# New places for background steps and a new order of attention's blocks in a two-network kernel

## The chip, the cores and the metric

The kernel runs on one core of one Trainium2 chip. The metric is device time in microseconds (us) of one execution, and the median of several executions is quoted. The trace was taken in one further execution, whose own time stands beside its span.

The engines are named as in the profile: PE (TensorE: matmuls and transposes), DVE (VectorE), ACT (ScalarE), POOL (GpSimd) and SP (SyncE, which issues most DMAs).

## What is computed

Two small networks run one after the other on 512 tokens of width 1024, all in float32. The first has a pooling mixer, a feed-forward layer, attention over a window of 128 tokens with shared keys and values, and a second feed-forward layer. The second network (an S5 mixer, an MLP, a state-space mixer, an MLP, a final norm) takes its output. Cut to what matters here:

```python
def conv_glu_ffn(h, w_in, conv_w, conv_b, w_out):          # twice: layer 0 and layer 1
    u = h @ w_in                                           # 1024 -> 2 x 2816
    u = sum(conv_w[k] * up[:, k:k + S] for k in range(3)) + conv_b
    gate, val = jnp.split(u, 2, axis=-1)
    return (gelu(gate) * val) @ w_out                      # 2816 -> 1024

def swa_sink_attention(q, kk, vv, sinks):                  # between the two
    s = einsum('bnqhgd,bnkhd->bnhgqk', q, kk)              # 4 token blocks x 4 groups of 4 heads
    p = exp(where(valid, s, -1e30) - m)
    return einsum('bnhgqk,bnkhd->bnqhgd', p, vv) / denom

# and for the second network, ahead of its time:
mod = silu(c) @ ada_w[0] + ada_b[0]                        # 1024 x 6144, one row
tables = f(s5_lambda, s5_log_dt, s5_b, s5_c, s5_d)         # the S5 mixer's tables, per group of states
```

## The kernel before

**Matmuls.** Each float32 product is made as three matmuls: activations and weights are split into a high and a low part (`hi`, `lo`; `wh`, `wl`). Weights come by DMA in chunks of 4 x 128 rows by 256 columns into `ws` (three buffers), ACT copies `wh` (L205) and DVE makes `wl` (L206), four buffers each. The matmuls are L220 to L222. PSUM tiles `mm` have four buffers.

**Feed-forward layer** (`ffn_layer`, L960). The 22 column tiles of the hidden width go in three phases, tiles 0 to 7, 8 to 15 and 16 to 21. In a phase each block of two tiles runs 96 matmuls of 512 columns for gate and value (tiles `h`), and then `glu`: DVE scales the four PSUM tiles (`u`, L969), ACT and DVE do the convolution (L974 to L976), ACT the gelu, DVE the product (L983) and the low part `lo` (L321). Tiles 0 and 1 are done ahead of the body. After the first and the second phase a down-projection (`project`) adds the phase's share of the output in four pairs of column tiles, and `evac` is called eight times. The third phase's down-projection is the layer's tail; it is done in two token halves of 256 columns, between which the next layer's norm is interleaved.

**Background.** `bg[0](n)` takes n steps of each generator that is registered (class `Background`). In layer 0 that is `s5_tables` (lines L560 to L793): it has 14 steps of small work, then, for each of 8 group blocks, two steps of phasors (L681 to L683) and five of matrices (L725 to L764), with a store (L780 to L793: ACT copies, PE transposes and matmuls `pb`, DMAs on ACT's queue) for each half of a group block. In layer 1 there are two generators, `ada_units` (two loads of 256 KB on POOL's queue, L495, and two DVE multiplies, L500, a step) and `s5_toeplitz`, short. What is left behind the body is drained at once: `end_tables` in layer 0, `work.drain()` in layer 1.

Steps are called at the body's start (2), after each block (`rate`: 5 in layer 0, 4 in layer 1) and after each evacuation of a down-projection (1).

**Attention** (`attention_layer`, `body_`). Sixteen blocks (g, n), g a group of four heads and n a block of 128 tokens. A block has `scores` (PE L1195 into the one buffer `sc`; DVE mask add L1198, maximum L1203, small ones L1204 and L1205; ACT exponentials L1207; DVE sum and reciprocal L1209 and L1210; POOL normalisation L1211), `turn` two blocks later (PE transposes L1219, copies to `pT`) and `values` three blocks later (PE L1237; `oh` and `ol`). `order` lists them: all groups with token blocks 0 and 1, then all with 2 and 3. Between the blocks `filler` takes steps of other PE work, as many as ATT_F says for that block: 12 steps of the query projections of groups 1 to 3 (`q_proj`, each a chunk of 12 matmuls of 512 columns, with a rotation L1111 to L1114 at the end of a half), then 8 steps of the output projection of the first token half (`o_proj(0)`), which may start when 8 blocks have their values. A group's scores need its `q_proj`; `o_proj(0)` needs all groups' token blocks 0 and 1.

**What sets the order.** The framework orders each engine's instructions by program order as priority, among those that are ready in its own model of time; the blocks of attention are moved up by 600 places (`high_priority`). On the chip each engine then runs its own list in order.

Of the kernel before, what the change touches and what calls it, by code (L numbers as in the profile page):

```python
# [31 lines left out]
POST_LAGS = (0, 1, 2, 3)  # L32
PRE_LAGS = (0, 1, 2)
MLP_HEAD, S5_HEAD = 2, 2
ATT_F = (3, 2, 2, 2, 2, 1, 0, 0, 0, 0, 0, 1, 1, 1, 1, 1, 1, 1, 1)
SSD_PLAN = (
# [26 lines left out]
def net_kernel(ctx: ExitStack, tc: tile.TileContext, I: dict, out: bass.AP, parts=ALL):  # L63
# [770 lines left out]
    bg = [no_bg]  # L834
# [125 lines left out]
    def ffn_layer(l, phases, late=None, rate=3):  # L960
# [52 lines left out]
        def body_():  # L1013
            hh, hl = S_["pre"].hi, S_["pre"].lo
            bg[0](2)
            for ph, (j0, j1) in enumerate(phases):
                final = ph == len(phases) - 1
                if final and late is not None:
                    late()
                for j in range(j0 if ph else 2, j1, 2):  # L1020
                    pp = {(i, q): psmm() for i in range(2) for q in range(2)}
                    src = [chunks(win, 0, KD, i * F1 + j * P) for i in range(2)]
                    if final and j == j1 - 2:
                        chs = [list(c) for c in src]
                        for q in range(2):
                            for i in range(2):
                                for ch in chs[i]:
                                    mm_chunk(pp[i, q], ch, q, hh, hl, KD, FULL)
                        for i in range(len(tl.runs)):
                            tl.load_apart(i)  # L1030
                    else:
                        for _ in range(2):
                            for i in range(2):
                                ch = next(src[i])
                                for q in range(2):
                                    mm_chunk(pp[i, q], ch, q, hh, hl, KD, FULL)
                    for q in range(2):
                        glu(j + q, *(scaled(pp[i, q]) for i in range(2)))
                    bg[0](rate)
                if not final:  # L1040
                    def evac(n, ps, span):
                        down(n, ps, span, ph == 0, False)
                        bg[0](1)

                    project(wout, j0, j1 - j0, 0, (0, 8), S_["ah"], S_["al"], evac)
                    S_["ah"], S_["al"] = [], []
# [36 lines left out]
    def attention_layer(cp, pa, C):  # L1083
# [101 lines left out]
        def body_():  # L1185
# [56 lines left out]
                A.activation(hi, pv, AF.Copy)  # L1242
                V.tensor_tensor(lo, pv, f(hi), ALU.subtract)

            order = [(g, n) for th in range(2) for g in range(4) for n in (2 * th, 2 * th + 1)]
            for _ in q_proj(0):
                pass
            work_ = [(q_proj(g), 0) for g in (1, 2, 3)] + [(o_proj(0), 8)]
            done = 0

            def filler():
# [7 lines left out]
            for i in range(16 + 3):  # L1259
                with tc.high_priority(offset=600):  # L1260
# [4 lines left out]
                    if 0 <= i - 3 < 16:  # L1265
                        values(*order[i - 3])
                        done += 1
                for _ in range(ATT_F[i]):
                    filler()
# [700 lines left out]
    for name in names:  # L1970
# [6 lines left out]
        if name == "ffn0":  # L1977
            layer = ffn_layer(0, ((0, 8), (8, 16), (16, 22)),
                              lambda: rope_c.update(rope_tables()) if "attn" in names else None, 5)
# [8 lines left out]
        elif name == "attn":  # L1988
            layer = attention_layer(opened("atc"), opened("atps", space=PSUM), rope_c or rope_tables())
            seam(prev, layer)  # L1990
            layer.body()
            close("atc", "atps")
        elif name == "ffn1":
            layer = ffn_layer(1, ((0, 8), (8, 16), (16, 22)), rate=4)
            seam(prev, layer)
            if tables_due:
                start_tables()
                end_tables()
                tables_due = False
            if ada_due[:1] == [0]:  # L2000
                start_ada(ada_due.pop(0))
            if toeplitz_due:
                work.gens.append(s5_toeplitz(opened("stz"), dr))
                toeplitz_due = False
            layer.body()
            work.drain()
            close("stz", "adp")
        else:
            if tables_due:
                start_tables()  # L2010
                end_tables()
                tables_due = False
            if toeplitz_due:
                work.gens.append(s5_toeplitz(opened("stz"), dr))
                toeplitz_due = False
            if ada_due and (name[-1] == "1" or name == "ssd" or ada_due[0] == 0):
                start_ada(ada_due.pop(0))
                work.drain()
                close("stz", "adp")
            if name == "s5":  # L2020
                layer = s5_layer(dr, opened("s5p"), opened("s5ps", space=PSUM))
            elif name == "ssd":
                layer = ssd_layer(opened("sdp"), dpl, opened("sdps", space=PSUM))
            else:
                layer = mlp_layer(int(name[-1]))
            seam(prev, layer)
            if name == "mlp0" and ada_due:
                start_ada(ada_due.pop(0))
            layer.body()
            work.drain()  # L2030
            close("adp", "s5p", "s5ps", "sdp", "sdps")
# [41 lines left out]
```

## Time and profile before

| | us |
|---|---|
| median of three executions | 2448.88 (2448.77 to 2451.74) |
| the profiled execution, its own time | 2448.6 |
| its span, first to last instruction | 2446.9 |
| PE busy | 2303.6 |
| DVE busy | 1707.1 |
| ACT busy | 1139.7 |
| POOL busy | 419.4 |
| layer 0's body from its first down-projection to the end of its last block | 162 to 417 |
| layer 0's tail, its first part | 417 to 444 |
| attention's blocks and the output projection of the first half | 540 to 661 |
| layer 1's body | 720 to 1037 |

Times in the rows count from the span's start. A PE row's duration includes what overlaps with the next matmul; matmuls of 512 columns follow each other at about 0.23 us. The clock column is the granted clock of TensorE: 1.0 is 2.4 GHz, 0.5 is 1.2 GHz. An idle time in square brackets stands before the row's instruction, with what ended it.

### The profile page before, as it was taken

The numbers are of one execution on the slowest core, as the hardware profiler recorded it, in microseconds if no ns is written. First come the engines' busy times: TensorE is split into PE (matmuls) and PEld (weight loads), VectorE is DVE, ScalarE is ACT, GpSimd is POOL, SyncE is SP. The second block draws the span as 40 slices with busy tenths as digits, with TensorE's granted clock in tenths as the row PEclk, the third lists the DMA queues.
The fourth block names the chain that finished last, engine by engine and source line by source line (L and its number), as shares of the span: only waits on it lengthen the run. The fifth ranks groups of instructions, "written<-read, shape, count | busy, mean of one in ns | idle before, by whom it ended". The sixth has DMA issues, their size and how long they took to land.

```text
span 2446.9 us, 33813 instructions
## 1 busy us (share of the span) xinstructions
PE 2303.6 (94%) x12477; PEld 1948.5 (80%) x12477; DVE 1707.1 (70%) x3064; ACT 1139.7 (47%) x2030; POOL 419.4 (17%) x596
## 2 busy tenths in 40 slices
PE   6989998788989999988799999999999999999998
PEld 6778877775878888787779878789878878888888
DVE  6896979767778697886646666666777788533333
ACT  6533535466675343455534333344555554422322
POOL 2001120002431211110301011010242340200110
PEclk9999999889989999989899999999999999999999
DMA  4224453311465655455742555542333332233322
GB/s 123 81 91 137 145 152 118 106 59 45 127 193 174 195 179 190 159 198 170 220 141 73 172 164 189 186 151 74 113 95 99 108 101 89 91 95 98 100 82 74
DMA packets 265190, 315.52 MB, mean 129 GB/s; under 512 B 34161, under 2 KB 222401, under 8 KB 264001
## 3 DMA queue, kind: packets, MB, share of 16 engines
q1 hardware_dynamic: 220929, 233.64, 30.5%
q0 software_dynamic: 19648, 62.41, 8.1%
q10 hardware_dynamic: 24448, 17.31, 2.2%
q8 instruction: 98, 1.61, 0.3%
q14 instruction: 67, 0.55, 0.1%
HBM read 289.12 MB, written 24.18 MB: 128 GB/s over the span
## 4 chain that ended last, share of the span: by engine, by line
PE 63%; DVE 14%; DMA 10%; issue 7%; ACT 4%; POOL 1%; SPq 0%; ACTq 0%; DVEq 0%; POOLq 0%
PE mm L221 18%; PE mm L220 18%; PE mm L222 18%; DMA as<-in_ada_w 6%; DVE wl L206 3%; DVE aa L500 1%; ACT wh L205 1%; PE pb L1746 1%; PE mm L1676 1%; PE mm L1677 1%; PE mm L1678 1%; DMA tz<-d_k 1%; DVE u L969 1%; PE py L1417 1%; DVE aa L514 1%
## 5 line engine op out<-in xcount | busy, mean ns | idle before, releaser
L220 PE MATMUL mm<-h,wh 128*128 128x512 f32 (+1 forms) x1792 | 665.6, 373 | 31.9 <-ACT h L429 16.2
L221 PE MATMUL mm<-h,wh 128*128 128x512 f32 (+1 forms) x1792 | 666.7, 373 | 7.4 <-DVE h L430 3.7
L222 PE MATMUL mm<-h,wl 128*128 128x512 f32 (+1 forms) x1792 | 663.4, 371 | 0.2 <-DVE wl L206 0.2
L205 ACT ACTIVATE wh<-ws 128x1024 fp32r<-128x1024 f32 (+1 forms) x367 | 387.1, 1059 | 505.6 <-PE mm L221 427.6
L206 DVE TENSOR_TENSOR wl<-ws,wh 128x1024 fp32r<-128x1024 f32 (+1 forms) x367 | 462.3, 1262 | 210.9 <-ACT wh L205 204.5
L220 PEld LDWEIGHTS mm<-h,wh 128*128 128x128 f32 x1792 | 346.2, 194 | 90.5 <-ACT h L429 17.4
L221 PEld LDWEIGHTS mm<-h,wh 128*128 128x128 f32 x1792 | 347.0, 194 | 64.9 <-DVE h L398 5.7
L222 PEld LDWEIGHTS mm<-h,wl 128*128 128x128 f32 x1792 | 346.9, 194 | 55.6 <-issue 1.8
L220 PE MATMUL mm<-hi,wh 128*128 128x512 f32 (+1 forms) x1056 | 371.5, 356 | 10.4 <-ACT wh L205 10.0
L221 PE MATMUL mm<-lo,wh 128*128 128x512 f32 (+1 forms) x1056 | 372.5, 354 | 3.4 <-DVE lo L321 3.0
L222 PE MATMUL mm<-hi,wl 128*128 128x512 f32 (+1 forms) x1056 | 372.1, 354 | 3.1 <-DVE wl L206 3.1
L220 PEld LDWEIGHTS mm<-hi,wh 128*128 128x128 f32 x1056 | 202.0, 192 | 38.4 <-ACT wh L205 11.4
L221 PEld LDWEIGHTS mm<-lo,wh 128*128 128x128 f32 x1056 | 202.2, 191 | 30.4 <-DVE lo L321 4.8
L222 PEld LDWEIGHTS mm<-hi,wl 128*128 128x128 f32 x1056 | 201.8, 191 | 30.1 <-DVE wl L206 4.0
L500 DVE SCALAR_TENSOR_TENSOR aa<-as,cond,aa 128x512 f32<-128x512 f32 x168 | 131.0, 780 | 112.0 <-DMA as<-in_ada_w 110.9
L1298 POOL TENSOR_TENSOR r<-r 128x512 f32<-128x512 f32 x64 | 87.7, 1374 | 670.7 <-ACT r L1294 484.3
L512 ACT ACTIVATE ab<-aa 128x512 bf16<-128x512 f32 x78 | 51.7, 662 | 118.1 <-DVE aa L500 81.1
L321 DVE TENSOR_TENSOR lo<-r,hi 128x512 fp32r<-128x512 f32 x64 | 47.2, 743 | 76.7 <-ACT hi L319 76.6
L495 POOL DMA_DIRECT2D as<-in_ada_w x96 | 51.6, 538 | 241.7 <-DVE aa L500 120.7
L1319 DVE SCALAR_TENSOR_TENSOR x<-mm,mod,x 128x512 f32<-128x512 f32 (+1 forms) x76 | 48.9, 662 | 58.4 <-PE mm L222 58.3
L319 ACT ACTIVATE hi<-r 128x512 fp32r<-128x512 f32 x64 | 40.4, 631 | 71.1 <-POOL r L1298 71.0
L297 DVE TENSOR_TENSOR acc<-acc,sq 128x256 f32<-128x256 f32 (+1 forms) x148 | 62.5, 440 | 9.3 <-ACT sq L296 5.2
(507 smaller groups left out, 3669.0 us busy)
## 6 DMA issues: line engine op xcount, KB each, us to landing
ws<-in_mlp_w SPq DMA_DIRECT2D x124, 512.0 KB, 4.0
ws<-in_ffn_w_in SPq DMA_DIRECT2D x88, 512.0 KB, 4.4
as<-in_ada_w POOLq DMA_DIRECT2D x96, 256.0 KB, 3.2
as<-in_ada_w SPq DMA_DIRECT2D x96, 256.0 KB, 3.4
ws<-in_m_w_in SPq DMA_DIRECT2D x41, 512.0 KB, 3.7
ws<-in_ffn_w_out SPq DMA_DIRECT2D x40, 512.0 KB, 3.4
ws<-in_w_o SPq DMA_DIRECT2D x16, 512.0 KB, 3.9
ct<-d_tab POOLq DMA_DIRECT2D x8, 1024.0 KB, 5.7
```

Source lines behind the costliest of these rows:

```text
L205: A.activation(h_, s_, AF.Copy)
L206: V.tensor_tensor(l_, s_, f(h_), ALU.subtract)
L220: T.matmul(ps, wh, xh, start=first, stop=False)
L221: T.matmul(ps, wh, xl, start=False, stop=False)
L222: return T.matmul(ps, wl, xh, start=False, stop=last).ins
L297: V.tensor_tensor(dst, dst, sq[:, a:b], ALU.add)
L321: return hi_, V.tensor_tensor(lo[:, ts], src, f(hi[:, ts]), ALU.subtract)
L495: queue.dma_start(st, W[k * P:(k + 1) * P, cb * 512:(cb + 1) * 512])
L500: V.scalar_tensor_tensor(acc, st, col(k), acc, ALU.mult, ALU.add)
L512: A.activation(pv[j], av, AF.Copy)
L1298: G.tensor_tensor(r, r, r, ALU.mult)
L1319: V.scalar_tensor_tensor(xT[n][:, ts], ps, md(i, 5, n), xT[n][:, ts], ALU.mult, ALU.add)
```

## The change

Three edits. In `ffn_layer` the steps behind the very last block of a layer go away, and each evacuation of the first two down-projections takes two steps instead of one; layer 1's rate goes from 4 to the default 3 (layer 0 keeps 5). In attention the blocks are taken in the order of ATT_ORDER, pairs of (group, token half): second halves of groups 0 and 1 come between first halves of later groups. ATT_F is changed to match: two projection steps in blocks 0 and 1, one in blocks 2 to 9, none in 10 to 13, and the output projection's eight in blocks 14 to 18. `o_proj(0)` may start when 12 blocks have their values.

```diff
-ATT_F = (3, 2, 2, 2, 2, 1, 0, 0, 0, 0, 0, 1, 1, 1, 1, 1, 1, 1, 1)
+ATT_ORDER = ((0, 0), (1, 0), (0, 1), (2, 0), (1, 1), (3, 0), (2, 1), (3, 1))
+ATT_F = (2, 2, 1, 1, 1, 1, 1, 1, 1, 1, 0, 0, 0, 0, 2, 2, 2, 1, 1)
...
-                    bg[0](rate)
+                    if not (final and j == j1 - 2):
+                        bg[0](rate)
                 if not final:
                     def evac(n, ps, span):
                         down(n, ps, span, ph == 0, False)
-                        bg[0](1)
+                        bg[0](2)
...
-            order = [(g, n) for th in range(2) for g in range(4) for n in (2 * th, 2 * th + 1)]
+            order = [(g, 2 * th + i) for g, th in ATT_ORDER for i in range(2)]
...
-            work_ = [(q_proj(g), 0) for g in (1, 2, 3)] + [(o_proj(0), 8)]
+            work_ = [(q_proj(g), 0) for g in (1, 2, 3)] + [(o_proj(0), 2 * ATT_ORDER.index((3, 0)) + 2)]
...
-            layer = ffn_layer(1, ((0, 8), (8, 16), (16, 22)), rate=4)
+            layer = ffn_layer(1, ((0, 8), (8, 16), (16, 22)))
```

## Rows read from the trace of the kernel before

**Rows 1.** The page, busy time and share of PE
```profile
PE 2303.6 (94%) x12477; PEld 1948.5 (80%) x12477; DVE 1707.1 (70%) x3064; ACT 1139.7 (47%) x2030; POOL 419.4 (17%) x596
```

**Rows 2.** Stretches: length, PE, PEld, DVE, ACT, POOL busy (instructions), clock, DMA share, GB/s
```profile
162.00:206.50 44.50, 44.39 (x204) 36.62 (x204) 36.19 (x63) 21.81 (x41) 9.21 (x16) 1.00 0.45 140
206.50:299.00 92.50, 92.50 (x453) 75.34 (x445) 80.11 (x135) 41.33 (x61) 16.86 (x28) 1.00 0.45 139
299.00:347.50 48.50, 47.25 (x237) 37.88 (x238) 44.46 (x77) 20.77 (x30) 7.12 (x12) 1.00 0.50 154
347.50:417.40 69.90, 69.88 (x338) 56.31 (x333) 58.86 (x105) 31.49 (x47) 11.97 (x50) 1.00 0.35 112
417.40:443.70 26.30, 14.82 (x91) 12.52 (x91) 26.05 (x47) 16.00 (x24) 1.82 (x4) 0.74 0.55 183
...
587.00:616.60 29.60, 19.70 (x120) 12.57 (x121) 22.18 (x52) 18.20 (x68) 8.61 (x5) 0.83 0.06 18
616.60:660.70 44.10, 44.10 (x350) 37.35 (x348) 30.67 (x53) 29.08 (x81) 23.56 (x24) 1.00 0.38 109
...
1036.60:1053.30 16.70, 11.21 (x77) 10.34 (x76) 15.22 (x21) 12.12 (x15) 1.67 (x4) 0.80 0.81 264
```

**Rows 3.** PE in order of time, layer 0's tail
```profile
419.81 0.39 PE L220 MATMUL mm<-hi,wh 128*128 128x256 f32 x1 [2.43 <-ACT wh L205]
...
443.69 0.39 PE L221 MATMUL mm<-lo,wh 128*128 128x256 f32 x1 [1.78 <-DVE lo L321]
```

**Rows 4.** Groups of DVE instructions by form, 417.4 to 443.7 us
```profile
L759 DVE TENSOR_TENSOR cp<-cp,ct 128x512 f32<-128x512 f32 x3 | 2.0, 682 | 0.0
...
L730 DVE TENSOR_SCALAR cc<-pb 128x128 f32<-128x128 f32 x1 | 0.3, 274 | 0.0
```

**Rows 5.** Layer 1's tail: DVE groups, 1036.6 to 1053.3 us, and PE's first row
```profile
L514 DVE TENSOR_TENSOR aa<-aa,ab 128x512 f32<-128x512 f32 x2 | 2.1, 1044 | 0.0
...
L498 DVE TENSOR_SCALAR aa<-as,mod 128x512 f32<-128x512 f32 x1 | 0.5, 485 | 0.6 <-ACT ab L512 0.6
...
1041.03 0.58 PE L220 MATMUL mm<-hi,wh 128*128 128x256 f32 x1 [4.42 <-ACT wh L205]
```

**Rows 6.** Line 495: the loads of `ada_units`, and what POOL waited for
```profile
L495 POOL DMA_DIRECT2D as<-in_s_w_in x16: 536/536/538, 1009.5 to 1064.2; - x16
...
  DVE aa L500: 149.5, 76
```

**Rows 7.** Layer 0's first phase: PE in order of time, and that stretch
```profile
137.95 0.77 PE L220 MATMUL mm<-h,wh 128*128 128x512 f32 x1 [6.06 <-DVE u L969]
...
131.50:142.20 10.70, 4.64 (x12) 3.41 (x11) 10.67 (x35) 4.10 (x5) 0.00 (x0) 0.68 0.14 49
```

**Rows 8.** PE in order of time, attention's stretch without projection steps
```profile
590.47 0.80 PE L1195 MATMUL sc<-kz,qr 64*128 64x128 f32 x4 [3.73 <-DVE qr L1114]
...
607.87 1.14 PE L1195 MATMUL sc<-kz,qr 64*128 64x256 f32 x8 [1.90 <-DVE s L1198]
608.93 1.10 PE L1219 MATMUL mm<-ident,s 128*128 128x128 f32 x8
```

**Rows 9.** DVE in order of time, the same stretch
```profile
600.86 0.16 DVE L1209 TENSOR_TENSOR st<-st 128x4 f32<-128x4 f32 x1 [2.10 <-ACT st L1208]
...
601.15 1.21 DVE L1198 TENSOR_TENSOR s<-sc,mask 128x1024 f32<-128x1024 f32 x1
...
606.60 1.21 DVE L1198 TENSOR_TENSOR s<-sc,mask 128x1024 f32<-128x1024 f32 x1
```

**Rows 10.** Lines 1211 and 1204: durations in ns, shortest/median/longest; POOL in order of time
```profile
L1211 POOL TENSOR_TENSOR s<-s,st x16: 1039/1893/2972, 555.6 to 642.4; 128x1024 f32<-128x1024 f32 x12, 128x512 f32<-128x512 f32 x4
...
L1204 DVE SCALAR_TENSOR_TENSOR st<-st,nsk x16: 147/154/1520, 550.7 to 638.6; 128x4 f32<-128x4 f32 x16
...
564.03 2.69 POOL L1211 TENSOR_TENSOR s<-s,st 128x1024 f32<-128x1024 f32 x1 [7.39 <-ACT oh L1242]
...
642.40 2.74 POOL L1211 TENSOR_TENSOR s<-s,st 128x1024 f32<-128x1024 f32 x1 [0.41 <-ACT f L1175]
```

## The prediction

> **What bounds the kernel now.** I read the page's engine totals first: TensorE (PE) is busy for 94% of the span [rows 1]. So a change can only be worth what PE loses: time in which it stands idle, and time in which its granted clock is 0.5 instead of 1.0 (1.2 instead of 2.4 GHz). The second view was busy time and clock by stretch, cut at the borders of the stages that the diff touches [rows 2]. In the long projections of both feed-forward layers PE is busy nearly all the time, so moving background work can win nothing there; it can only do harm. Two kinds of stretch do lose. At the end of a feed-forward layer, between the last up-projection matmul and the moment when the last activation tile `lo` is ready, layer 0 takes 26.30 us with PE busy 14.82 at clock 0.74, and layer 1 takes 16.70 us with 11.21 busy at 0.80. In attention, 587.0 to 616.6 us has PE busy 19.70 of 29.60 at clock 0.83, while the stretch behind it is full (44.10 of 44.10). Third, I read the timelines to see who ends those gaps, below.
>
> **Ends of the feed-forward layers.** In layer 0 PE's first tail matmul waits 2.43 us for `wh`, and a later one 1.78 us for `lo` [rows 3]. VectorE (DVE) is busy for 26.05 of these 26.30 us [rows 2]. Sixteen of its groups in that stretch belong to the background tables and sum to 14.6 us (the first and the last of them in [rows 4]): about half of what DVE does there is not what PE waits for. They come from `bg[0](5)` behind the last block and from four more steps that only the drain takes. The counts: the generator of the tables needs 72 calls. Before, the body of layer 0 gives 2 + 3x5 + 8 + 4x5 + 8 + 3x5 = 68. After, it gives 2 + 15 + 16 + 20 + 16 = 69 by the end of the second down-projection, so the first block of the last phase takes the remaining 3, and blocks 18 and 20 and the drain take none.
>
> What is the end then worth? The same code in layer 1, with only 4.05 us of background on DVE (three groups, 2.1 + 1.5 + 0.5, the first and the last in [rows 5]), gets from the last matmul to the last `lo` in 16.7 us. I take layer 1's end as the size of layer 0's new end: 26.3 - 16.7 = 9.6 us shorter. PE does about equal tail work in both: in layer 0, 13.7 us (2 x 0.26 x 26.3) run at half clock, with some 8.4 of them busy, so 14.8 busy is 10.6 of full-speed work, of which 2.4 are table matmuls (estimates from the rows). Those 2.4 us must be done elsewhere, in stretches where PE is full. Net gain 7.2 us. Bounds: nothing, if the wait for the weight DMA alone sets the end; 12 us if the end falls below layer 1's.
>
> Layer 1's own end: its rate falls from 4 to 3, each down-projection evacuation takes two steps instead of one, and the last block none. Steps of the modulation generator (60 calls): before 14 + 8 + 16 + 8 + 12 = 58 and 2 in the drain; after 11 + 16 + 12 + 16 = 55 by the end of the second down-projection and 60 after block 18. But it cannot go at any pace: it has two buffers, its loads on POOL's queue wait for DVE's multiply (149.5 us in all), and DVE waits for the loads; the last load is issued at 1064.2 us, 28 us after the up-projection's end [rows 6]. So it will lag as now and end somewhat earlier than 1064 rather than at block 18. I take the 4.05 us on DVE as removed, and PE's 4.42 us gap [rows 5] shortened by about that, with half of its half-clock stretch left: gain 4 us, bounds -2 (its waits move in front of the down-projections' adds) to 6.
>
> **What the moved steps cost where they go.** Seven table steps (one group block) hold 18 DVE instructions of 0.68 us and ten small ones of about 0.28 [rows 4]: 15.0 us by durations, 2.1 a step. Durations overlap in the records (the 26.05 us that DVE is busy in layer 0's end hold 31 us of them), so a step costs DVE about 1.8 us. Each of layer 0's two down-projections gets 8 more steps, 14 to 16 us. DVE has 8.3 us free in the first (36.19 of 44.50), 12.4 in the second up-projection (80.11 of 92.50), 4.0 in the second down-projection (44.46 of 48.50) and 11 in the third up-projection, which gives up 12 steps [rows 2]. So the first overflow of about 7 fits the following up-projection, and the second of about 11 runs on into the third, which has 11 + 22 us for it. Background issued earlier is due earlier than the next block's splits, so part of that overflow lands ahead of `wl` and `u` in DVE's queue, with PE behind them. ACT and POOL also get the steps' copies and DMA issues, but neither is over half busy there. What such a jam costs has a row: in the first phase, where DVE is full, PE waits 6.06 us for `u` and resumes at half clock [rows 7]. Bounds 0 (all deferred) to 12 us (the second overflow in full). I take 4, nearer to nothing, because the second up-projection is full on DVE to 87% and PE loses nothing there.
>
> **Attention.** Before, all first halves (token blocks 0 and 1 of the four groups) come first, so blocks 2, 4 and 6 each need a new query projection, and the output projection can start after block 7. After, second halves fill in: new projections are needed at blocks 2, 6 and 10, twelve projection steps lie in blocks 0 to 9, blocks 10 to 13 have none, and the output projection's eight steps come from block 14 on. Nothing is added or removed on any engine; only PE's cover changes. In the bare stretch PE waits 3.73 us for the last group's rotated queries and then for DVE's mask add, 1.90 us and more a block [rows 8]: DVE stands 2.10 us at the sum of the block before, because ACT isn't done, with the next mask add behind it in its queue [rows 9]. That pace, 5.4 us from one mask add to the next, against 1.14 + 1.10 us of scores and transposes and about as much again as one of them for the values, 3.3 us of PE work, is what projection steps should cover. After, the bare blocks are four instead of about five and a half (blocks 6 to 12 are issued in the bare stretch, the first of them still beside rope work), but the wait for the last rope and the latency from scores to values stay, and the output projection now waits for block 11 instead of 7. PE's loss in the stretch is 9.9 idle plus about 4 of half clock [rows 2]; I give back a quarter to a third of it, 4 us. Bounds: 10 (all idle covered) and -6 (output projection later by its latency, with the bare stretch as long as now).
>
> Here a rule speaks against the change. The rows: POOL's normalisation takes 1.89 us on 1024 columns in the median and up to 2.97, and a DVE instruction on four columns that takes 0.154 us took 1.52 us once, beside one of them. Company of POOL with DVE's two-input instructions thus costs about 1.4 us on DVE and 0.8 to 1.1 on POOL; four of the twelve long normalisations take over 2.6 us, the first and the last of these at 564.03 and 642.40 us, and none lies in the bare stretch [rows 10]. The Trainium skill, SBUF — State Buffer, section "Who interferes with whom", says that a DVE instruction with two SBUF inputs contends with a GpSimd instruction that reads SBUF, and that the one which comes second is blocked for the whole instruction. By that rule, with which this trace agrees, spreading rope and weight splits over ten blocks makes more such meetings; by the rows alone they are rare enough to leave out of the sum.
>
> **The sum**, against the profiled execution (2448.6 us, span 2446.9; the median is 0.3 above it): layer 0's end -7.2, moved steps +4, attention -4, layer 1's end -4: -11.2, so 2437 us. The span should fall equally, as what lies around it (1.7 us) isn't touched.
>
> **Rivals.**
> 1. *No change* (2445): projection steps are already issued where PE has room, so attention only shifts its idle time (0 instead of -4), and the moved steps cost 8 instead of 4: -7.2 - 4 + 8 is about -3. For it: PE is full from 616.6 us on whatever stood before. Against it: the 14.6 us of tables in layer 0's end.
> 2. *Slower* (2459): DVE overflows in layer 0's second down-projection and its backlog stands ahead of the third phase's splits. PE waits the full 12 us, resumes at half clock and loses again as in [rows 7], 6.06 plus about 3.4 for 0.32 x 10.7 us of clock: +21.5, less 7.2 and 4, is about +10. It decides where DVE's need in the down-projection (44.5 + 14) exceeds its 48.5 us and nothing is deferred.
> 3. *The port* (2443): four more meetings of 1.4 us on DVE, all on the mask chain, turn attention's -4 into +2. This is the case in which the rule of the Trainium skill (SBUF — State Buffer) named above comes to bear.
> 4. *More* (2427): the bare stretch closes (10 us instead of 4) and the moved steps cost nothing.
>
> **How the numbers follow.** Forecast 0.52, no change 0.12, slower 0.13, port 0.10, more 0.13. Between 2424 and 2450 lie all but the slower rival and tails: over 8 in 10. About 0.2%, 4.9 us, is what a measurement of this kernel can tell from no change. Faster: 0.48 of the forecast's 0.52, more, and half of the port: 0.66. Same: 0.04 of the forecast, the other half, and no change: 0.20. Slower: 0.14.
>
> **What would show it.** Right: no table instruction on DVE in layer 0's end, which lasts 15 to 18 us; DVE busy for over 95% of layer 0's second down-projection; a gap of 2 to 3 us instead of 4.42 in layer 1's end; in attention a bare stretch under 25 us. Wrong: new PE waits over 2 us for `wl` or `u` at the start of layer 0's third phase; a bare stretch of 30 us or more that only lies later; normalisations over 2.6 us in more than eight blocks; or a change of more than 3 us outside these three layers, for which this prediction has no term.

## The result and the profile after

The changed kernel takes 2493.94 us (median, 2488.49 to 2495.95), beside 2450.31 us for the kernel before on the same chip: a ratio of 1.0169, 95% interval 1.0144 to 1.0194 (ratios here and below are taken over all executions, so they differ a little from the quotient of the two medians). It is slower by 1.7%, where the prediction was 2437 us, faster by 0.5%. The profiled execution took 2495.95 us with a span of 2494.3, 47.4 us longer than the span before.

Where these 47.4 us lie is read by cutting both traces at the same borders of the stages. The third column of times is the kernel with layer 0's part of the change alone, which comes back below.

| stretch | before | after | difference | layer 0's part alone |
|---|---|---|---|---|
| up to layer 0's first down-projection (no edit there) | 162.0 | 167.1 | +5.1 | 164.1 |
| layer 0: down, up, down, up | 255.4 | 259.5 | +4.1 | 259.6 |
| layer 0's end | 55.4 | 37.5 | -17.9 | 37.1 |
| attention | 212.7 | 221.1 | +8.4 | 206.3 |
| layer 1: start and first up-projection | 104.5 | 100.8 | -3.7 | 98.2 |
| layer 1: first down-projection | 45.3 | 44.9 | -0.4 | 46.6 |
| layer 1: second up-projection | 89.1 | 115.6 | **+26.5** | 89.0 |
| layer 1: second down-projection | 44.9 | 44.8 | -0.1 | 45.2 |
| layer 1: third up-projection | 67.3 | 94.5 | **+27.2** | 68.0 |
| layer 1's end | 46.3 | 45.1 | -1.2 | 46.9 |
| the rest | 1364.0 | 1363.4 | -0.6 | 1362.1 |

Two stretches of layer 1 hold 53.7 us, more than the whole loss. These are the busy times by stretch after (columns as in [rows 2]): layer 0's second down-projection, its end, attention, layer 1's second and third up-projections and its end.

```profile
306.50:356.40 49.90, 48.35 (x246) 38.66 (x245) 48.85 (x88) 22.74 (x33) 11.99 (x20) 1.00 0.54 165
426.60:464.10 37.50, 36.37 (x298) 35.67 (x297) 26.45 (x60) 17.46 (x37) 0.00 (x0) 1.00 0.27 85
464.10:685.20 221.10, 188.16 (x1176) 152.47 (x1175) 155.04 (x323) 146.99 (x373) 48.84 (x58) 0.90 0.31 88
830.90:946.50 115.60, 93.66 (x447) 74.89 (x446) 83.74 (x126) 43.53 (x58) 20.68 (x39) 0.90 0.52 161
991.30:1085.80 94.50, 70.03 (x337) 55.64 (x335) 66.71 (x100) 35.41 (x46) 16.62 (x31) 0.87 0.45 149
1085.80:1130.90 45.10, 37.85 (x299) 37.29 (x298) 27.18 (x48) 19.25 (x27) 2.13 (x4) 0.92 0.47 153
```

The same view of before, for layer 0's end, attention, layer 1's second and third up-projections and its end (the down-projection stands in [rows 2]):

```profile
417.40:472.80 55.40, 43.88 (x338) 40.66 (x338) 39.50 (x80) 26.03 (x50) 3.46 (x7) 0.88 0.40 131
472.80:685.50 212.70, 183.40 (x1184) 151.47 (x1185) 159.24 (x346) 147.68 (x382) 49.07 (x52) 0.92 0.29 87
835.30:924.40 89.10, 88.85 (x430) 72.69 (x428) 75.27 (x112) 40.85 (x55) 16.09 (x30) 1.00 0.58 182
969.30:1036.60 67.30, 67.02 (x317) 54.16 (x315) 55.41 (x87) 27.50 (x38) 12.35 (x23) 1.00 0.50 162
1036.60:1082.90 46.30, 39.63 (x318) 38.26 (x317) 35.68 (x59) 24.88 (x32) 8.39 (x16) 0.93 0.59 196
```

Before, PE (the first number behind the length) stood idle for 0.25 and 0.28 us in layer 1's second and third up-projections. After, it is idle for 21.94 and 24.47 us there and its clock has fallen to 0.90 and 0.87 on the mean. Of the 53.7 us, 45.9 are this idle time; the other 7.8 are PE's busy time, which grew from 88.85 to 93.66 and from 67.02 to 70.03 us at the lower clock. No other engine is full in these stretches; DVE has 83.74 of 115.60 us.

What PE waits for is seen in its timeline. After, at the end of the second up-projection's first block (columns: start, duration, engine, line, operation, tiles, count, and in brackets the idle time before it with its releaser):

```profile
858.09 0.25 PE L485 MATMUL pn<-one,ab 128*128 128x1 bf16 x4 [1.14 <-ACT ab L513]
859.56 0.27 PE L485 MATMUL pn<-one,ab 128*128 128x1 bf16 x4 [1.22 <-ACT ab L513]
876.37 0.27 PE L485 MATMUL pn<-one,ab 128*128 128x1 bf16 x4 [16.54 <-ACT ab L513]
876.50 0.77 PE L221 MATMUL mm<-h,wh 128*128 128x512 f32 x1
877.07 0.63 PE L222 MATMUL mm<-h,wh 128*128 128x512 f32 x1
```

And in the third up-projection:

```profile
1014.90 0.39 PE L223 MATMUL mm<-h,wl 128*128 128x512 f32 x1
1021.05 0.27 PE L485 MATMUL pn<-one,ab 128*128 128x1 bf16 x4 [5.76 <-ACT ab L513]
...
1024.17 0.27 PE L485 MATMUL pn<-one,ab 128*128 128x1 bf16 x4 [1.12 <-ACT ab L513]
1039.62 0.27 PE L485 MATMUL pn<-one,ab 128*128 128x1 bf16 x4 [15.19 <-ACT ab L513]
```

L485 (L484 before) is `total`: three times four matmuls of one column that sum a finished column block of the modulation over the partitions. Four of them take 0.27 us, but they stand in PE's own list, and everything behind them waits with them. The rows at 859.56 and 1024.17 are the last four of one column block, those at 876.37 and 1039.62 the first four of the next, and no matmul of the layer stands between: PE has nothing that it may do. When it goes on, a layer matmul takes 0.63 us instead of 0.39. The sums of these waits, from 830 to 1090 us after and from 830 to 1040 us before (us in total, times, longest):

```profile
PE pn L485 <- ACT ab L513: 46.4, 10, 16.5
```

```profile
PE pn L484 <- ACT ab L512: 0.7, 2, 0.4
```

The stream that feeds these totals is the loads `as` of `ada_units`. After, in the last column blocks before the first wait and during it (POOL's issues; first and last start):

```profile
L496 POOL DMA_DIRECT2D as<-in_ada_w x24: 536/536/538, 800.0 to 856.3; - x24
L496 POOL DMA_DIRECT2D as<-in_ada_w x8: 536/537/538, 860.9 to 875.9; - x8
```

Three rounds of eight loads start at 800.0 and are followed by the next at 860.9: 20.3 us for a round, which is what one column block needs, and 5.1 us for a step of two loads. PE's wait of 16.54 us, 859.83 to 876.37, covers one more round. (The issues run two loads ahead of the multiplies: the round from 860.9 on holds the last six loads of the block that PE waits for, whose eight multiplies on DVE run from 860.16 to 875.65, and the first two of the next.) The rest of the machine is quiet in it:

```profile
860.00:876.00 16.00, 0.00 (x0) 0.00 (x0) 6.36 (x12) 0.32 (x1) 3.82 (x8) 0.50 0.44 135
```

DVE is busy for 6.36 of 16 us. So it isn't a jam of DVE; it is a stream with two buffers that was asked for steps faster than it can make them. A doubled evacuation asks for two steps (10.2 us of stream) in 44.9 / 8 = 5.6 us. By count: from the start of the first doubled down-projection (786.0) to the end of the wait (876.4) are 90.4 us; the 16 steps of that down-projection need 81 us, and with the three of the block behind it 97.

### The profile page after: what moved, and what is told of

Same layout as the page of the kernel before. It is cut to its first block, busy times and chain, and to the rows that moved or that the text cites. A ratio compares the mean times of both kernels' runs of the same rounds, so it can differ in the third digit from the quotient of the medians.

```text
span 2494.3 us, 33844 instructions
## 1 busy us (share of the span) xinstructions
PE 2314.1 (93%) x12477; PEld 1952.1 (78%) x12477; DVE 1715.5 (69%) x3064; ACT 1144.0 (46%) x2030; POOL 417.8 (17%) x596
## 4 chain that ended last, share of the span: by engine, by line
PE 65%; DVE 11%; DMA 10%; issue 9%; ACT 4%; POOL 1%; SPq 0%; ACTq 0%; DVEq 0%; POOLq 0%
PE mm L222 19%; PE mm L221 19%; PE mm L223 19%; DMA as<-in_ada_w 7%; DVE wl L207 3%; ACT wh L206 1%; DVE aa L501 1%; DMA as<-in_s_w_in 1%; PE pb L1749 1%; PE mm L1679 1%; PE mm L1680 1%; PE mm L1681 1%; DMA ws<-in_ffn_w_out 1%; POOL tz L803 1%; PE py L1420 0%
```

## The experiments

The theory is that this stream, run ahead of its pace by layer 1's doubled steps, costs some 50 us; that layer 0's edit is a gain; and that attention's edit is a loss. First each part was done or undone alone.

**One part at a time.** Layer 1's part undone in the changed kernel, and layer 1's part alone in the kernel before:

```diff
-                    if not (final and j == j1 - 2):
+                    if not (final and j == j1 - 2 and l == 0):
...
-                        bg[0](2)
+                        bg[0]((2, 1)[l])
...
-            layer = ffn_layer(1, ((0, 8), (8, 16), (16, 22)))
+            layer = ffn_layer(1, ((0, 8), (8, 16), (16, 22)), rate=4)
```

> The changed kernel with layer 1's feed-forward put back as it was (four background steps a block, one a down-projection evacuation, steps behind the last block too); layer 0's edit and attention's new order stay. Theory: the loss is made in layer 1's own second and third phases, where the doubled steps let the modulation stream fall behind and PE then waits in its own order for that stream's column totals (21.9 and 24.5 us of idle PE). So both phases are back at 89 and 67 us, and the time is the changed kernel's less 26.5 + 27.2 - 3.3 = 50 us: 2440 to 2447 us. Rival, that attention's new order or layer 0's edit shifts something into layer 1: the phases stay over 100 and 80 us, and the time over 2480 us.

Measured: 2446.3 us, ratio to before 0.9975 (0.9965 to 0.9986). The second and third up-projections are back at 89.1 and 67.7 us, and PE's wait for the totals over both is one of 0.7 us.

> The kernel before with layer 1's part alone: three steps a block instead of four, two an evacuation, none behind the last block; layer 0 and attention as before. Theory: both waits for the modulation stream come back in full, about 26 and 27 us longer second and third phases, 3 us less in the first: 46 to 52 us slower than before, 2496 to 2502 us. Rival, that the loss needs layer 0's or attention's edit as well: less than 20 us slower.

Measured: 2502.66 us, ratio 1.0212 (1.0193 to 1.0231), 2.1% slower and just above the range. The two up-projections take 115.7 and 96.7 us, and PE's waits there are

```profile
PE pn L484 <- ACT ab L512: 47.3, 12, 15.8
```

So layer 1's part is both sufficient and necessary for the 50 us; neither attention nor layer 0 has a share in it.

Layer 0's part alone:

```diff
-                    bg[0](rate)
+                    if not (final and j == j1 - 2 and l == 0):
+                        bg[0](rate)
...
-                        bg[0](1)
+                        bg[0]((2, 1)[l])
```

> The kernel before with layer 0's part alone: two table steps a down-projection evacuation and none behind the last block; layer 1 and attention as before. Theory: layer 0's end is 17.9 us shorter, and its other phases give back 3 to 4 us: 12 to 16 us faster than before, 2434 to 2438 us. Rival, that the table steps moved into full stretches cost what they free: within 5 us of before.

Measured: 2427.44 us, ratio 0.9911 (0.9886 to 0.9936); once more on another chip:

> Layer 0's part alone once more, in more rounds and on the same chip as the kernel beside it. Theory: 2424 to 2432 us, 0.7 to 1.1% faster than before. Rival, that the first measurement's chip flattered it: within 0.5% of before.

Measured: 2427.48 us, ratio 0.9900 (0.9883 to 0.9916). That is 22 to 25 us, more than the 12 to 16 expected. Layer 0's end and attention behind it:

```profile
423.70:460.80 37.10, 36.19 (x299) 35.59 (x298) 26.44 (x61) 17.11 (x36) 0.00 (x0) 1.00 0.27 86
460.80:667.10 206.30, 179.73 (x1177) 148.71 (x1176) 155.31 (x328) 145.18 (x376) 45.53 (x50) 0.94 0.30 87
```

Layer 0's end has lost 18.3 us and runs at full clock with 0.9 us of idle PE. Attention, whose code is as before, is 6.4 us shorter. Its first norm no longer finds DVE late: the norm's first instruction (`acc`, ACT) starts 24.8 us ahead of attention's border instead of 4.0, and PE idles for 1.7 of attention's first 8.2 us, where before it idled for 6.3 of the first 8.4. Before, PE's waits in attention hold 3.4 us for `acc` and 2.2 for `dg`, of which 0.8 for `dg` are left. Another 6.3 us came where nothing had been edited, at layer 1's start with its first up-projection (104.5 to 98.2 us); that is told at the end.

Attention's part alone:

```diff
+ATT_ORDER = ((0, 0), (1, 0), (0, 1), (2, 0), (1, 1), (3, 0), (2, 1), (3, 1))
-ATT_F = (3, 2, 2, 2, 2, 1, 0, 0, 0, 0, 0, 1, 1, 1, 1, 1, 1, 1, 1)
+ATT_F = (2, 2, 1, 1, 1, 1, 1, 1, 1, 1, 0, 0, 0, 0, 2, 2, 2, 1, 1)
...
```

> The kernel before with attention's new order and its new spread of projection steps, and nothing else. Theory: attention itself got longer, 212.7 to 221.1 us, by gaps that are now spread over blocks 0 to 9 (waits for DVE's mask add and rope) and a bare stretch that only lies later: 6 to 10 us slower than before, 2456 to 2460 us, and no wait in layer 1. Rival, that attention's loss in the changed kernel came from layer 0's shorter end (a different clock or different weight arrivals at attention's start): within 3 us of before.

Measured: 2468.5 us, ratio 1.0070 (1.0048 to 1.0092), some 17 us slower, twice what the theory gave. Attention is 233.2 us long, 20.5 more than before:

```profile
476.40:709.60 233.20, 193.21 (x1183) 156.96 (x1182) 160.25 (x346) 150.61 (x383) 48.87 (x58) 0.88 0.30 84
```

With layer 0's edit in both, it is 221.1 against 206.3: 14.8 more. The 8.4 us that the changed kernel showed were this loss less the 6.4 that layer 0's edit brings to the same stretch.

**Loads or multiplies?** The stream's step holds two loads and two multiplies on DVE, and either could set its pace. In the changed kernel every second load was left out, and then, in another kernel, seven eighths of each multiply but the first of a column block. These two kernels, and two more below for which no interval is given, have one run each, beside 2453.24 us for the kernel before:

```diff
+                if k % 2 == 0 or queue is not nc.gpsimd:
                     st = pool.tile([P, 512], F32, tag="as", bufs=2, name=nm("as"))
                     queue.dma_start(st, W[k * P:(k + 1) * P, cb * 512:(cb + 1) * 512])
```

> The changed kernel in which layer 1's modulation stream leaves out every second load and multiplies the tile loaded before it once more (so its modulation values are wrong); all its multiplies, splits and totals stay. Theory: the stream is paced by its loads, two in flight with 2.8 to 5.2 us each from issue to landing. In the changed kernel eight loads take 16.5 us, 4.1 us a step, and a down-projection evacuation asks for two steps every 5.6 us, so 8 x (8.2 - 5.6) = 21 us of backlog, which is the idle time seen (21.9 and 24.5 us). With half the loads two steps need about 4.1 us, under 5.6: no backlog, PE's idle time in the second and third up-projections under 4 us together, 2436 to 2448 us. Rival, that VectorE's queue is what the stream waits in: the idle stays above 15 us in each phase, about 2490 us.

Measured: 2436.4 us. The view of waits has no row of PE over the second and third up-projections, which take 89.5 and 67.3 us.

```diff
-                    V.scalar_tensor_tensor(acc, st, col(k), acc, ALU.mult, ALU.add)
+                    w = 64 if queue is nc.gpsimd else 512
+                    V.scalar_tensor_tensor(acc[:, :w], st[:, :w], col(k), acc[:, :w], ALU.mult, ALU.add)
```

> The changed kernel in which layer 1's modulation stream multiplies 64 of 512 columns of each loaded tile instead of all (so its modulation values are wrong); all its loads stay. That takes about 0.5 of 0.68 us from each of its multiplies on VectorE. Theory: the loads pace the stream, but the buffer of a load is free only after the multiply, so a step falls from 4.1 to about 3.6 us and the backlog from 21 to about 8 x (7.2 - 5.6) = 13 us: 10 to 18 us of idle PE in each of the two up-projections, 2468 to 2484 us. Rival, that VectorE's load is the cause: the idle falls under 5 us in each, 2440 to 2450 us.

Measured: 2485.25 us, a little above the range. The long waits are 14.62 and 13.99 us, and their sum over both stretches is

```profile
PE pn L485 <- ACT ab L514: 34.7, 12, 14.6
```

against 46.4: a multiply of 0.28 instead of 0.75 us takes a quarter off the waits and leaves the rest, while half the loads leave nothing. The loads are the larger part of the step's 5.1 us; the multiply counts because the buffer is free only behind it. A third part was left alone in both kernels: the accumulator `aa` has one buffer, so between the last multiply of a column block (ended at 835.81 in the changed kernel) and the first of the next (839.63), while ACT and DVE split it, no multiply can start. That is 3.8 of the 20.3 us of a round. Four load buffers instead of two, or a second accumulator, would be the direct tests; no run has them.

**What is asked for, or where it is asked?** If the cost is work that the stream still owes, fewer steps in the down-projections must only move it. The changed kernel with one step an evacuation in layer 1 (`bg[0]((2, 1)[l])`; three a block and none behind the last block stay):

> The changed kernel with one step instead of two at each of layer 1's evacuations; three steps a block and none behind the last block stay. Theory: one step needs 4.1 us and an evacuation gives 5.6, so no backlog and no wait in the second and third up-projections (89 and 67 us). But only 45 of the 60 steps are then asked for before the layer's last block, and the rest, 30 loads of about 2.07 us, or 62 us, are issued at the layer's end (45 us) and behind it: PE waits there instead, 10 to 60 us, or, if the end's own matmuls stand ahead of those totals, the waits come only at the next layer's start. 2445 to 2500 us, with the loss in another place. Rival, that what costs is the doubled step in the down-projections whatever the stream still holds: all waits gone, 2440 to 2446 us.

Measured: 2475.72 us. In the two up-projections (88.7 and 66.8 us) the totals make no wait. They come behind the last matmul of the layer, as the theory has it:

```profile
1068.32 0.28 PE L223 MATMUL mm<-hi,wl 128*128 128x256 f32 x1
1080.91 0.27 PE L485 MATMUL pn<-one,ab 128*128 128x1 bf16 x4 [12.32 <-ACT ab L513]
...
1100.13 0.27 PE L485 MATMUL pn<-one,ab 128*128 128x1 bf16 x4 [14.66 <-ACT ab L513]
```

36.3 us in six waits. So both too many steps and too few cost, in different places.

**A better pace.** I then took layer 0's part and, in layer 1, five steps a block, one an evacuation and none behind the last block, at the 4.1 us a step that I had read from the loads during a wait:

> The kernel before with layer 0's part of the change (two table steps an evacuation) and, in layer 1, five steps a block, one an evacuation and none behind the last block; attention as before. Theory: a step needs 4.1 us, a block of the up-projections gives about 22 and an evacuation 5.6, so five and one never fall behind, and all 60 steps are asked for by block 18: no wait for the totals in the up-projections (89 and 67 us), and layer 1's end without its stream: 40 to 45 instead of 46.3 us, not layer 0's 37, because its first wait is for a weight load and not for VectorE. Against layer 0's part alone (2427.4 us) 0 to 6 us less: 2420 to 2428 us, 1.0 to 1.4% faster than before. Rival, that any faster pace makes the totals wait: the up-projections longer by over 5 us, and the time over 2432 us.

Measured: 2453.2 us, ratio 1.0008 (0.9998 to 1.0018). The theory's number was wrong and the rival right: over layer 1 from its second up-projection on,

```profile
PE pn L484 <- ACT ab L512: 21.9, 6, 11.1
```

The 4.1 us came from the eight loads within one round, without the gap to the next. By whole column blocks a step takes 5.1 us, and a block of the up-projection (89.1 / 4 = 22.3 us) has room for 4.4 of them, an evacuation (5.6) for 1.1. By this count four and one, as before, is the fastest pace that whole steps allow. It also makes luck of the agreement in the text on half the loads: 8 x (8.2 - 5.6) = 21 us was near the idle time of 21.9 and 24.5 us, but with 10.2 us for two steps the same sum gives 37. The backlog isn't paid in one place; the blocks behind a down-projection, with three steps in 22.3 us, work some of it off. With 5.0 us a step the next kernel, which only drops the steps behind layer 1's last block (`rate=4`, one an evacuation):

> The kernel before with layer 0's part of the change, and in layer 1 only the steps behind the last block taken out (four a block and one an evacuation stay). Theory, mended after five a block fell behind too: when it is asked to run without pause, the stream needs 20.1 us for a column block of four steps (loads from 804.3 to 884.6 us in the changed kernel for 32 loads), so 5.0 us a step, not 4.1. Four and one ask for 24 steps or 120 us in a phase of 136, and never fall behind; 54 of 60 steps are asked for by the last block, and the 6 of the drain, 30 us, run beside the 40 us of matmuls of the layer's end, in whose order the totals stand behind them. No wait in the up-projections, the layer's end within 3 us of 46.9: 2421 to 2431 us, equal to layer 0's part alone within 0.3%. Rival, that the drain's totals make PE wait at the end: 6 to 20 us more.

(The count in that text is off: the row from 804.3 us on has 30 loads up to 875.9. From 800.0 to 860.9 there are 24, which gives 5.1 instead of 5.0.) Measured: 2425.42 us, ratio 0.9897 (0.9881 to 0.9913), beside 0.9900 (0.9883 to 0.9916) for layer 0's part alone on the same chip: equal, as expected, and both 1.0% faster than the kernel before. The totals make 2.7 us of waits in five places, the longest 0.8, and layer 1's end takes 46.9 us. Steps taken out behind layer 1's last block are worth nothing that can be measured.

**Attention: order or spread?** The new order of blocks with the old spread of steps:

```diff
+ATT_ORDER = ((0, 0), (1, 0), (0, 1), (2, 0), (1, 1), (3, 0), (2, 1), (3, 1))
 ATT_F = (3, 2, 2, 2, 2, 1, 0, 0, 0, 0, 0, 1, 1, 1, 1, 1, 1, 1, 1)
...
```

> The kernel before with attention's new order of blocks but the old spread of projection steps (three, two, two, two, two, one, then none for five blocks). With order and spread both new, attention was 233.2 us long, 20.5 more than before. Theory: the spread is what costs, since one step a block leaves stretches in which scores follow one another with nothing between them while VectorE works off rope and mask adds; with the old spread the query projections are done early as before, and attention is within 5 us of 213. Rival, that the order costs (second-half blocks, twice the work of a first block, come while projections still run): attention stays over 225 us.

Measured: 2457.11 us (one run beside 2453.24), and attention is 213.7 us long, against 212.7 before and 233.2 with the spread as well:

```profile
476.80:690.50 213.70, 181.46 (x1177) 149.14 (x1176) 159.17 (x339) 146.28 (x374) 49.67 (x58) 0.92 0.30 89
```

So, with the new order, the spread of one step a block costs the 15 to 20 us, and the order by itself nothing that one run can tell. (The new spread can't be had with the old order: there block 4 needs 8 of the 12 projection steps, and the new spread has given 6.) A last try kept the order, the early query projections and the new spread of the output projection, on top of the kernel with five steps a block:

> The same kernel with attention's new order of blocks, the old spread of the query projections (3, 2, 2, 2, 2, 1, then none) and the new spread of the output projection (2, 2, 2, 1, 1 from block 14 on). With the order alone attention was 213.7 us against 212.7. Theory: order and output spread are worth little, since the projections set the cover: attention within 4 us of the other kernel's, the time within 0.2%. Rival, that the second halves between first halves do fill the bare stretch once the projections come early: 4 to 10 us faster.

Measured: 2458.94 us, ratio 1.0028 (1.0017 to 1.0038), where its neighbour had 1.0008. Attention takes 208.2 us against 206.3. The second halves don't fill the bare stretch; order and output spread together cost 0.2%, if anything, and so the loss lies in the spread of the query projections.

What the spread does is seen in the waits of PE in attention: changed kernel, then layer 0's part alone, whose attention is the old one (us in total, times, longest).

```profile
PE sc L1197 <- DVE s L1200: 12.0, 8, 4.1
PE mm L1221 <- POOL s L1213: 3.3, 4, 1.2
PE sc L1197 <- DVE qr L1116: 2.5, 1, 2.5
```

```profile
PE mm L1220 <- POOL s L1212: 6.7, 6, 2.5
PE sc L1196 <- DVE s L1199: 4.4, 1, 4.4
PE sc L1196 <- DVE qr L1115: 3.7, 1, 3.7
```

The scores' wait for the mask add of the block before (the scores have one buffer) is 4.4 us in one place with the old order and spread, 7.6 in seven with the new order alone, and 12.0 in eight with both (11.8 in seven with attention's part alone). That is only a part of the loss. From the new order alone to order and spread, attention grew by 19.5 us (213.7 to 233.2): PE's idle time by 7.8, from 32.2 to 40.0, and its busy time by 11.8, from 181.46 to 193.21, at a mean clock of 0.88 instead of 0.92. So more than half of the loss is slower work of PE and not waiting. One of the scores' waits, in the changed kernel's timelines of PE and DVE:

```profile
528.55 1.13 PE L1197 MATMUL sc<-kz,qr 64*128 64x256 f32 x8
532.59 0.49 PE L1197 MATMUL sc<-kz,qr 64*128 64x128 f32 x4 [2.91 <-DVE s L1200]
535.59 0.80 PE L1197 MATMUL sc<-kz,qr 64*128 64x128 f32 x4 [2.50 <-DVE qr L1116]
```

```profile
528.74 0.48 DVE L198 SCALAR_TENSOR_TENSOR wl<-ws,vec,wh 128x256 fp32r<-128x256 f32 x1
...
530.06 1.27 DVE L198 SCALAR_TENSOR_TENSOR wl<-ws,vec,wh 128x256 fp32r<-128x256 f32 x3
531.25 0.15 DVE L1206 SCALAR_TENSOR_TENSOR st<-st,nsk 128x4 f32<-128x4 f32 x1
531.32 1.22 DVE L1200 TENSOR_TENSOR s<-sc,mask 128x1024 f32<-128x1024 f32 x1
```

Weight splits for the coming projection step stand ahead of the mask add in DVE's list. And one step a block isn't what PE's list holds. Further on, three blocks' scores follow one another with no projection between, two of them waiting for DVE:

```profile
572.25 1.14 PE L1197 MATMUL sc<-kz,qr 64*128 64x256 f32 x8
...
574.79 1.13 PE L1197 MATMUL sc<-kz,qr 64*128 64x256 f32 x8 [0.38 <-DVE s L1200]
580.01 2.08 PE L1197 MATMUL sc<-kz,qr 64*128 64x256 f32 x8 [4.09 <-DVE s L1200]
...
582.78 0.77 PE L221 MATMUL mm<-h,wh 128*128 128x512 f32 x1
```

The step meant to cover them comes behind. That this is so because the blocks are moved ahead by 600 places is argued; no run changed the priorities.

## Why the prediction was wrong

**Layer 1's evacuations: the step that failed.** The prediction wrote of `ada_units` that it has two buffers, cannot go at any pace and "will lag as now". The mechanism was on the table, and [rows 6] had the lag. What was missing is the question who waits for a lagging stream. I looked for its price only on DVE (4.05 us in layer 1's end) and not on PE, where its totals stand. A lag that is free while PE's list meets each total late enough costs its full length once PE meets it early. Nor did I compare demand with pace: two steps an evacuation against 5.6 us. The sum has no term for PE in layer 1's second and third up-projections; there the measured cost is +53.7 us, and no rival had it. The slower rival put its jam in layer 0's DVE, where a step is multiplies and copies; there, the doubled steps did no such harm.

For PE's list the Trainium skill has the rule (PSUM — Partial Sum Buffer, section "Engine vs sequencer instructions"): a weight load may overlap matmuls that are under way, but matmuls start and complete in program order. The trace agrees: from 859.83 to 876.37 us no matmul of the layer ran, though its inputs had nothing to do with the stream.

**Layer 0's end: direction right, size low.** Predicted 9.6 us shorter, with 2.4 us of table matmuls going elsewhere; measured 17.9, beyond the bound of 12; 16.7 of them lie in the part that the text sized, from the last up-projection matmul to the last `lo` (26.3 to 9.6 us). The model for its new size was layer 1's end, and that carries a wait of its own: 4.42 us for `wh` [rows 5], 4.65 in the kernel with layer 0's part alone, 6.61 in the changed kernel, where ACT waits 3.92 us for a weight load. Layer 0's new end has 1.1 us of idle PE in all. The last `lo` is ready at 436.2, 9.6 us behind the last up-projection matmul, not 15 to 18. No table instruction is left in the end, as predicted. What I left out besides: the late end also delayed the norm at attention's start; attention is another 6.4 us shorter without it.

**Moved steps: near in size, wrong in parts.** Predicted 2.4 us of table matmuls and +4 of waits in layer 0's other phases, 6.4 together; measured +4.1. Nearly all of it is PE's busy time, 254.02 us before and 257.95 after (3.9 more, with 1270 instead of 1214 instructions). DVE is busy for 48.85 of 49.90 us in the second down-projection (the text asked for over 95%), but the only wait of PE over 0.2 us in these phases is one of 1.55 us for `lo`, where before one of 1.2 stood. So the waits came to about nothing and the moved work on PE to more than 2.4 us; that the total is near is luck. No wait for `wl` or `u` came at the third phase's start. A full DVE cost nearly nothing; PE met nothing there that stood behind the tables.

**Attention: wrong sign.** Predicted -4 within -6 to +10 of gain; the edit costs 15 to 20 us. The text reckoned with four bare blocks instead of five and a half, and took for granted that a projection step called in each block is executed in each. It isn't, and the bare stretch lasts 26.8 us after (592.7 to 619.5) against 29.2 with the old order and spread (both with layer 0's edit), while the stretch ahead of it gets new gaps.

**The port: fell.** The rival expected more normalisations of POOL in company, the case for the rule in the Trainium skill (SBUF — State Buffer, "Who interferes with whom"). Before, the longest took 2.97 us [rows 10] and the longest of DVE's four-column instructions beside them 1.52; after, the latter is 0.88 us, and no normalisation takes over 1.89:

```profile
L1213 POOL TENSOR_TENSOR s<-s,st x16: 1039/1893/1894, 536.0 to 630.7; 128x1024 f32<-128x1024 f32 x12, 128x512 f32<-128x512 f32 x4
```

**Layer 1's end.** Predicted -4 with a gap of 2 to 3 us; it is -1.2, and the gap grew from 4.42 to 6.61 us, since it hangs on a weight load and not on DVE. Without the last steps, but with the old pace, the end took 46.9 us: nothing gained.

**Outside the three layers.** The text named a change of over 3 us there as a sign against it. The +5.1 before layer 0's first down-projection is such a one, but kernels with the same code in that stretch began their up-projection anywhere between 53.1 and 56.8 us, so it says nothing of the change. A slip in the chances, on which nothing rests: those of *same* add up to 0.21 and not 0.20.

Of the sum, then: -11.2 was forecast. Layer 0 alone is worth -22 to -25, attention +15 to +20, layer 1 some +50; together +40 to +48, and +41.5 (1.69%) is measured. The first outweighs the second, and the third decides.

## What to carry to other kernels

Before moving background steps, work out the pace of the stream they ask for (here 5.1 us a step, by whole column blocks, gaps included) and compare it with the time between the calls; then find every instruction of that stream in the in-order list of the engine that sets the end. A lag without a price now is no licence to make it longer: ask at which instruction the critical engine will meet it. And a step that is called between two blocks runs there only if the priorities leave it there; look at the engine's list.

## What was not expected

**A quiet machine doesn't speed up a stream of two loads.** In the wait from 860 to 876 us, with the DMA engines busy for 0.44 of the time, instead of 0.62 from 800 to 860, and PE idle, a round of eight loads took 15.0 us from the first issue to the last (860.9 to 875.9); in the three rounds ahead of it, beside busy matmuls, the same took 15.6 to 15.9 us.

**An edit in layer 0 shortened layer 1's start by 6.3 us.** Before, two waits of PE of 4.80 and 4.70 us stood there; with layer 0's part alone they are 1.84 and 0.90. ACT before, and then in the kernel with layer 0's part alone:

```profile
698.04 2.05 ACT L805 ACTIVATE th<-tz 128x1024 f32<-128x1024 f32 x1 [3.96 <-DMA tz<-d_k]
700.49 0.51 ACT L429 ACTIVATE h<-x,vec 128x256 fp32r<-128x256 f32 x1 [0.40 <-ACT th L805]
```

```profile
679.09 0.51 ACT L429 ACTIVATE h<-x,vec 128x256 fp32r<-128x256 f32 x1 [3.46 <-DVE x L448]
681.22 2.10 ACT L805 ACTIVATE th<-tz 128x1024 f32<-128x1024 f32 x1 [0.90 <-DMA tz<-d_k]
```

Before, a copy of the background's second generator stood ahead of the first `h` in ACT's list and waited 3.96 us for its own DMA; with layer 0's edit the two have changed places, presumably because layer 0 is shorter in the framework's model of time. That would be the same fault as the totals on PE, in small. But no kernel has only these two exchanged, and with attention's part alone the start takes 99.3 us as well, though there a copy ahead of the first `h` waits 4.23 us for its DMA. So the copy's share of the 6.3 us is argued, not shown.
